# Two-layer decoder trunk on one core: the instruction order made with the framework's timeline simulation

## The chip, the cores and the metric

The kernel runs on one core of a Trainium2 chip, as one program with one launch. The metric is the device time in microseconds, as the median of several runs. A core has five engines with a queue of instructions each: TensorE (PE in the profile, with its weight loads as PEld), VectorE (DVE), ScalarE (ACT), GpSimd (POOL) and SyncE (SP). Each queue is worked off strictly in the order in which it was written into the program, and engines wait for each other by semaphores. SP and POOL also issue the DMA transfers here.

## The reference

The reference is a trunk of two layers on 512 tokens of width 1024. Layer 0 mixes tokens by multi-head latent attention, layer 1 by a gated linear recurrence (HGRN2). Cut to what matters:

```python
for i in range(2):
    h = mla_mixer(x, ...) if i % 2 == 0 else hgrn2_mixer(x, ...)
    x = layer_norm(ALPHA * x + h, ln_mix_g[i], ln_mix_b[i])
    hh = x @ ffn_w_in[i]                       # 1024 -> 2 * 2816
    g, u = hh[..., :2816], hh[..., 2816:]
    x = layer_norm(ALPHA * x + (silu(g) * u) @ ffn_w_down[i], ln_ffn_g[i], ln_ffn_b[i])
    x = x + sigmoid(x @ ple_w_gate[i]) * (p[i] @ ple_w_proj[i])
```

## The kernel before

Tokens lie in four tiles of 128 (NT), the width in eight chunks of 128 (KC). Every factor of a product is kept as two fp32r parts, a high part (`hi`, a rounded copy made by ACT in `split`, L179) and a low part (`lo`, source minus `hi`, made by DVE, L180, or for some weights by POOL), and `mm3` (L200 to L202) multiplies hi by hi, hi by lo and lo by hi.

The work of a layer runs in stages: the mixer; its output projection with the layer norm (`out_proj`, `ln_finish`, L330 to L344); the first product of the feed-forward part (`gate_up`); the second one (`ffn`, the "down" product); the gated embedding (`ple`).

`gate_up` handles 2 of the 22 column blocks in the plain way and 20 per layer (`block`, 40 in all) by a 2x2 block product with seven products in place of eight. One such product is 12 matmuls of 256 columns. In program order a block does: product into bank A; ACT copies A out (L439); product into B; product into C and its copy (L439); a further product accumulated into A, which must come after the copy of A was made; then more of the same kind. ACT and DVE also prepare the weights of the blocks to come (`prep`, L391 to L407): passes of ACT over 1024 columns (L184, L185, twice L179), and two over 512.

The down product (`ffn`) is such a block product too, over six blocks `b` of the inner dimension, five of size 2 and one of size 1, in the order 0, 1, 5, 2, 3, 4. Its first half makes, for each block, four weight operands: `b11` as it is, and `t1`, `t2`, `t3`, which are differences of the weight blocks made in a chain:

```python
r11 = load(0, 0, b)                                # L504, SP: DMA into a "raw" tile (3 slots)
...
t1 = mid(b, "ma")                                  # a tile of tag "ma" (5 slots)
minus(t1, r11, src(0, 1, b))                       # L509 ACT: t1 = -r11; L510 POOL: DMA adds a weight block to it
w1 = made(t1, b)                                   # L179 ACT, L180 DVE: its two parts (whi, wlo)
...
minus(t2, t1, src(1, 1, b))                        # L509, L510 again, on t1
w2 = made(t2, b)
...
t3 = mid(b, "ma")
v.tensor_tensor(out=t3, in0=t2, in1=r11, op=ALU.subtract)   # L558, DVE
w3 = made(t3, b)
```

So t1 needs a DMA that adds into it, t2 a second such DMA after the first has landed, and t3 needs t2. After that the block's 48 matmuls of 512 columns follow (24 in the block of size 1). The second half, which reuses t2, and the layer norm come behind. (The first t2 lies in a tile of tag "ma" as well and is held until the second half; the later ones have tiles of tag "big".)

What sets the order of the work: nobody writes it out. The kernel is traced as a program in the order of its Python code, and the framework's `TileContext` then makes the queues of all engines on leaving the `with` block. It plays the program through on a simulated machine; whenever an engine there is free, it takes the earliest instruction in program order whose inputs are there and for whose output tile a slot is free. An instruction may so pass earlier ones that are still waiting. In the order that came out for this kernel, instructions do pass each other on ACT, DVE, POOL and PE, but the first writers of the tiles of any one tag ("raw", "ma", "whi" and so on) stand in program order without an exception. On the chip the order is fixed; the semaphores that keep it right are put in by the framework.

Lines that the change and the prediction touch: L1099 (`TileContext`), L179, L180, L184, L185, L186, L200 to L202, L210, L304, L344, L439, L504, L509, L510, L558.

## Time and profile before

| | |
|---|---|
| median of 3 runs (lowest to highest) | 1341.29 us (1335.26 to 1345.14) |
| the profiled execution: its own time, its span | 1340.34 us, 1338.5 us |
| TensorE: matmuls busy, weight loads busy | 1267.8 us (95%), 1120.8 us (84%) |
| VectorE, ScalarE, GpSimd busy | 912.3, 751.9, 196.4 us (68%, 56%, 15%) |
| mean granted TensorE clock | 0.985 |
| moved by DMA | 173.77 MB, 130 GB/s on average |

A busy TensorE is not one at its peak: matmuls overlap, and one that waits inside its own record counts as busy. So a stage's speed is read from the number of matmuls in a stretch of time beside its busy time. The rows of a table by stretches give, in this order: the stretch, its length, the busy time and (in brackets) the count for PE, PEld, DVE, ACT and POOL, then the granted clock, the share of the DMA engines and the GB/s. A row of a timeline gives the start, the duration, the engine, the source line, the operation, output and input, and in square brackets the idle time before it with what ended it.

### The profile page before, as it was taken

How to read it: one execution, taken by the hardware profiler on the slowest of the kernel's cores; microseconds unless marked ns; L12 is line 12 of the kernel's file. 1: busy time of each engine (PE TensorE's matmuls, PEld its weight loads, DVE VectorE, ACT ScalarE, POOL GpSimd, SP SyncE). 2: the span in 40 equal slices, each digit the busy share in tenths (PEclk: the TensorE clock that was granted, in tenths of full speed). 3: DMA queues.
4: the chain of work that ended last, by engine and by line, in shares of the span. 5: the costliest groups of instructions: out<-in, count | busy, mean ns of one | idle time of the engine just before them, and what ended most of it. 6: DMA issues, size and time to landing. Idle time of an engine off the chain costs nothing.

```text
span 1338.5 us, 20202 instructions
## 1 busy us (share of the span) xinstructions
PE 1267.8 (95%) x7768; PEld 1120.8 (84%) x7768; DVE 912.3 (68%) x1608; ACT 751.9 (56%) x1276; POOL 196.4 (15%) x215
## 2 busy tenths in 40 slices
PE   8999999999999779899999999999999998978998
PEld 8787889999998558688888887889999998756787
DVE  7988397777757559843377776359677774747863
ACT  6666267776756557433334434247667765556652
POOL 0200131111211111100002220023211111111100
PEclk9999999999999889899999999999999999988999
DMA  6213128787876668421311221315887885676821
GB/s 221 80 48 127 62 65 205 186 192 174 184 161 118 113 142 228 146 96 63 127 63 63 64 87 35 99 63 152 212 180 182 186 185 110 114 127 154 236 95 48
DMA packets 53378, 173.77 MB, mean 130 GB/s; under 512 B 6305, under 2 KB 6561, under 8 KB 53025
## 3 DMA queue, kind: packets, MB, share of 16 engines
q1 hardware_dynamic: 34848, 117.94, 27.2%
q0 software_dynamic: 18432, 54.53, 23.8%
q8 instruction: 61, 1.00, 0.3%
q14 instruction: 37, 0.30, 0.1%
HBM read 170.35 MB, written 2.10 MB: 129 GB/s over the span
## 4 chain that ended last, share of the span: by engine, by line
PE 66%; DMA 10%; issue 9%; DVE 8%; ACT 5%; POOL 1%; SPq 0%; POOLq 0%; DVEq 0%; ACTq 0%
PE ps L200 16%; PE ps L201 16%; PE ps L202 16%; DMA big<-ffn_w_down 3%; DMA raw<-ffn_w_in 3%; PE sc L200 2%; PE sc L201 2%; PE wg L201 2%; PE sc L202 2%; PE wg L200 2%; PE wg L202 2%; DMA ma<-ffn_w_down 2%; DMA raw<-ple_w_proj 2%; PE tp L304 2%; PE sc L942 2%
## 5 line engine op out<-in xcount | busy, mean ns | idle before, releaser
L200 PE MATMUL ps<-big,whi 128*128 128x256 f32 (+1 forms) x768 | 237.3, 309 | 0.7 <-DVE part L459 0.7
L202 PE MATMUL ps<-big,wlo 128*128 128x256 f32 (+1 forms) x768 | 237.0, 309 | 0.0
L201 PE MATMUL ps<-big,whi 128*128 128x256 f32 (+1 forms) x768 | 235.8, 307 | 0.0
L200 PE MATMUL ps<-whi,big 128*128 128x512 f32 (+2 forms) x528 | 208.6, 395 | 6.2 <-ACT whi L179 6.2
L201 PE MATMUL ps<-wlo,big 128*128 128x512 f32 (+2 forms) x528 | 205.8, 390 | 4.0 <-DVE wlo L180 3.9
L202 PE MATMUL ps<-whi,big 128*128 128x512 f32 (+2 forms) x528 | 205.1, 388 | 0.0
L179 ACT ACTIVATE whi<-raw 128x1024 fp32r<-128x1024 f32 (+1 forms) x103 | 104.7, 1022 | 102.3 <-PE ps L202 35.7
L180 DVE TENSOR_TENSOR wlo<-raw,whi 128x1024 fp32r<-128x1024 f32 (+1 forms) x91 | 108.3, 1192 | 73.5 <-ACT whi L179 71.9
L200 PEld LDWEIGHTS ps<-big,whi 128*128 128x128 f32 x768 | 147.3, 192 | 5.7 <-DVE part L459 0.9
L201 PEld LDWEIGHTS ps<-big,whi 128*128 128x128 f32 x768 | 147.2, 192 | 5.4
L202 PEld LDWEIGHTS ps<-big,wlo 128*128 128x128 f32 x768 | 147.1, 192 | 5.2
L180 DVE TENSOR_TENSOR wlo<-ma,whi 128x1024 fp32r<-128x1024 f32 (+1 forms) x68 | 81.1, 1192 | 64.0 <-ACT whi L179 64.0
L200 PEld LDWEIGHTS ps<-whi,big 128*128 128x128 f32 x528 | 101.1, 192 | 26.2 <-ACT whi L179 8.3
L201 PEld LDWEIGHTS ps<-wlo,big 128*128 128x128 f32 x528 | 101.2, 192 | 25.4 <-DVE wlo L180 7.4
L202 PEld LDWEIGHTS ps<-whi,big 128*128 128x128 f32 x528 | 100.8, 191 | 19.1
L179 ACT ACTIVATE whi<-ma 128x1024 fp32r<-128x1024 f32 (+1 forms) x68 | 69.7, 1025 | 39.4 <-DMA ma<-ffn_w_down 28.7
L186 POOL DMA_DIRECT2D ma<-ffn_w_in x40 | 34.7, 869 | 233.6 <-DVE big L460 144.1
L210 POOL TENSOR_TENSOR rr<-rv,mhalf 128x1 f32<-128x1 f32 (+2 forms) x28 | 26.7, 952 | 235.7 <-DVE rv L208 235.7
L200 PE MATMUL sc<-whi,big 128*128 128x512 f32 (+1 forms) x104 | 42.1, 408 | 14.6 <-ACT whi L179 14.6
L439 ACT ACTIVATE part<-ps 128x256 f32<-128x256 f32 x120 | 44.0, 372 | 20.1 <-PE ps L202 20.1
L180 DVE TENSOR_TENSOR mb<-ma,mb 128x1024 fp32r<-128x1024 f32 x40 | 48.9, 1223 | 6.3 <-ACT mb L179 3.4
L180 POOL TENSOR_TENSOR wlo<-raw,whi 128x1024 fp32r<-128x1024 f32 x12 | 29.6, 2475 | 152.1 <-ACT whi L179 152.1
(329 smaller groups left out, 3222.5 us busy)
## 6 DMA issues: line engine op xcount, KB each, us to landing
raw<-ffn_w_in SPq DMA_DIRECT2D x88, 512.0 KB, 4.7
wlo<-ffn_w_in POOLq DMA_DIRECT2D x40, 512.0 KB, 7.1
raw<-ffn_w_down SPq DMA_DIRECT2D x30, 512.0 KB, 4.1
ma<-ffn_w_in POOLq DMA_DIRECT2D x40, 256.0 KB, 6.8
mb<-ffn_w_down POOLq DMA_DIRECT2D x20, 512.0 KB, 6.3
raw<-ple_w_gate SPq DMA_DIRECT2D x16, 512.0 KB, 3.5
raw<-hgrn_w_fq SPq DMA_DIRECT2D x16, 512.0 KB, 3.5
ma<-ffn_w_down POOLq DMA_DIRECT2D x12, 512.0 KB, 5.6
```

Source lines behind the costliest of these rows:

```text
L179: self.nc.scalar.activation(hi, src, AF.Copy)
L180: (eng or self.nc.vector).tensor_tensor(out=lo, in0=src, in1=hi.bitcast(F32), op=ALU.subtract)
L186: self.nc.gpsimd.dma_start(lo, src, accum_op=ALU.add)
L200: mm(ps, a[0], b[0], start=start, stop=False, skip_group_check=more)
L201: mm(ps, a[0], b[1], start=False, stop=False, skip_group_check=more)
L202: mm(ps, a[1], b[0], start=False, stop=stop, skip_group_check=more)
L210: nc.gpsimd.tensor_tensor(out=r, in0=v, in1=self.mhalf[:, :n], op=ALU.pow)
L304: self.nc.tensor.transpose(out=ps[:, c * P:(c + 1) * P], in_=src[:, c * P:(c + 1) * P], identity=self.ident)
L439: copy = lambda dst, src: nc.scalar.activation(dst, src[:, :N], AF.Copy)
L942: nc.tensor.matmul(ps[:, c * P:(c + 1) * P], X[:, c * P:(c + 1) * P], pair_view(cs[0][:, :, 1, :], cs[1][:, :, 0, :]), start=True, stop=True)
```

## The change

One argument of `TileContext` is added. It tells the framework to play the program through on another simulated machine, its timeline simulation, when it makes the queues. The traced program is the same: the same instructions with the same operands, tiles, tags and numbers of slots, in the same program order. What may differ is the order of the instructions on each engine, and with it the semaphores and the slot that each tile gets.

```diff
-    with tile.TileContext(nc) as tc:
+    with tile.TileContext(nc, schedule_with_timeline_sim=True) as tc:
         trunk(tc, ins, out)
```

## The prediction

> **What bounds the kernel now.** I read the page from the top, then the chain of waits, then tables by stretches, to see in which stage time is lost at all.
>
> ```profile
> PE 1267.8 (95%) x7768; PEld 1120.8 (84%) x7768; DVE 912.3 (68%) x1608; ACT 751.9 (56%) x1276; POOL 196.4 (15%) x215
> ...
> PEclk9999999999999889899999999999999999988999
> ...
> PE 66%; DMA 10%; issue 9%; DVE 8%; ACT 5%; POOL 1%; SPq 0%; POOLq 0%; DVEq 0%; ACTq 0%
> ```
>
> TensorE is the bound: 95% busy, two thirds of the chain that ended last. A new order adds and removes no work, so it can only shorten or lengthen the rest: time in which PE starves. Where is that? The table by stretches compares stages in which nothing but PE counts with the down product's first half:
>
> ```profile
> 267.60:368.10 100.50, 100.50 (x840) 100.50 (x839) 74.70 (x124) 71.29 (x122) 17.70 (x21) 1.00 0.81 184
> 970.30:1104.20 133.90, 133.90 (x1118) 133.90 (x1117) 100.32 (x165) 93.74 (x161) 22.64 (x26) 1.00 0.81 184
> 635.74:669.20 33.46, 33.46 (x149) 27.74 (x148) 11.89 (x11) 12.61 (x16) 0.00 (x0) 1.00 0.39 127
> 440.00:500.00 60.00, 45.58 (x161) 33.16 (x160) 32.35 (x43) 34.10 (x45) 8.68 (x10) 0.89 0.66 132
> 1160.00:1220.00 60.00, 45.50 (x167) 33.59 (x166) 30.43 (x40) 31.26 (x41) 9.56 (x11) 0.88 0.64 122
> ```
>
> The first two rows are the block products of gate_up in both layers: PE is busy throughout, with a matmul of 256 columns every 100.50 / 840 = 0.120 us, while DVE and ACT are busy 74% and 71%. No order makes this faster. The third row, plain products of 512 columns, gives PE's pace there: 33.46 / 149 = 0.225 us. The last two rows are the down product's first half, also 512 columns: 161 matmuls at that pace need 36.2 of the 60 us, 167 need 37.6. So PE loses 23.8 + 22.4 = 46.2 us in these two stretches, about a third of it (13.8 us, the 0.11 and 0.12 missing from the clock times 60) as a lower clock. That is the one large loss which an order could touch.
>
> **Why PE starves there.** DVE's timeline has the instruction that makes t3 (L558), once for each block:
>
> ```profile
> 442.31 0.69 DVE L558 TENSOR_TENSOR ma<-big,raw 128x512 f32<-128x512 f32 x1 [1.79 <-DMA big<-ffn_w_down]
> 458.31 1.23 DVE L558 TENSOR_TENSOR ma<-big,raw 128x1024 f32<-128x1024 f32 x1 [5.52 <-DMA big<-ffn_w_down]
> 474.18 1.23 DVE L558 TENSOR_TENSOR ma<-big,raw 128x1024 f32<-128x1024 f32 x1 [4.87 <-DMA big<-ffn_w_down]
> 491.58 1.23 DVE L558 TENSOR_TENSOR ma<-big,raw 128x1024 f32<-128x1024 f32 x1 [7.14 <-DMA big<-ffn_w_down]
> ```
>
> The period is 16.0, 15.9 and 17.4 us, where 48 matmuls need 10.8. ACT's and POOL's timelines show what fills one period:
>
> ```profile
> 442.37 0.63 ACT L179 ACTIVATE whi<-big 128x512 fp32r<-128x512 f32 x1 [2.99 <-DMA big<-ffn_w_down]
> 442.90 1.04 ACT L509 ACTIVATE ma<-raw 128x1024 f32<-128x1024 f32 x1
> 444.35 0.87 POOL L510 DMA_DIRECT2D ma<-ffn_w_down  x1 [5.18 <-DVE t L543]
> 450.48 1.06 ACT L179 ACTIVATE whi<-ma 128x1024 fp32r<-128x1024 f32 x1 [3.97 <-DMA ma<-ffn_w_down]
> 451.44 1.04 ACT L509 ACTIVATE big<-ma 128x1024 f32<-128x1024 f32 x1
> 452.89 0.87 POOL L510 DMA_DIRECT2D big<-ffn_w_down  x1 [5.12 <-DVE wlo L180]
> 458.31 1.06 ACT L179 ACTIVATE whi<-big 128x1024 fp32r<-128x1024 f32 x1 [2.24 <-DMA big<-ffn_w_down]
> 459.28 1.04 ACT L509 ACTIVATE ma<-raw 128x1024 f32<-128x1024 f32 x1
> ```
>
> Two adding DMAs stand one behind the other: t1 is negated at 442.90 and landed at 450.48; t2 is negated at 451.44 and landed at 458.31; then the next block's t1 is negated at 459.28. Between the blocks nothing overlaps. The reason is the tag "ma": t1 of the next block and t3 of this one come from it, t3 stands earlier in the program, and the first writers of a tag keep program order. So the next t1 can't start before L558 has its turn, and L558 waits for t2's DMA. Both simulated machines hand out slots from the same program, so I take this chain to survive the change.
>
> **The change part by part.** No instruction is added or removed, so the sum is made of displacements, against the profiled execution's own 1340.34 us (span 1338.5 us; 0.95 us under the median).
>
> *Saturated stages* (gate_up's blocks, the row products, HGRN): 0. What hides a displaced pass there is PE's queue of further products; the price if that cover goes is the second rival.
>
> *The chain in the down product*: the same instructions in the same chain, 0. What a new order could still do is swap ACT's two passes at each landing. Above, t2's negation starts 451.44 - 450.48 = 0.96 us after t1 has landed and the next t1's 459.28 - 458.31 = 0.97 us after t2, because the split of the landed weight goes first. Three full periods in each of two layers, 1.93 us each: 11.6 us gained if both negations go first everywhere, and a bound of +12.7 us (two passes of 1.06 us in six periods) if another pass is put ahead each time. The earlier instruction wins where both are ready, and both become ready with the same landing; so 0, with -11.6 and +12.7 kept for the range.
>
> *Borders at the layer norms*: here PE waits for one vector instruction after another.
>
> ```profile
> PE tp L304 <- DVE big L344: 10.3, 6, 3.9
> ...
> L180 DVE TENSOR_TENSOR wlo<-raw,whi 128x1024 fp32r<-128x1024 f32 (+1 forms) x91 | 108.3, 1192 | 73.5 <-ACT whi L179 71.9
> ...
> L661 ACT ACT_TABLE_LOAD x2 | 2.6, 1283 | 7.8 <-PE ps L202 7.8
> ```
>
> PE's transposes wait 10.3 us in all, in six places, for the layer norm's last step; that is what a perfect order could save. A weight split of 1.19 us that slips ahead in each of the six costs 7.2 us. Such a slip frees the weights of the stage behind earlier by as much, so I set 0 between -10.3 and +7.2. ACT's function tables are reloaded where functions mix, 1.28 us each; the trace has eight loads, and I bound what a new mix adds by four, 0 to +5.1, and take 0. Queues of SP and POOL: SP's loads are issued in program order, tag "raw", and stay; POOL's adding DMAs go with the chain above.
>
> **The sum** is 1340.3 + 0, or 1341 at the median's level, between 1340.3 - 11.6 - 10.3 = 1318 and 1340.3 + 12.7 + 7.2 + 5.1 = 1365 if all terms fall on one side.
>
> **The rivals.**
>
> *Faster: the chains overlap.* If the timeline simulation lets a later block's t1 start before this block's t3, the stage falls to PE's pace: -46.2, 1294 us. For it: raw tiles are loaded well ahead, and ACT stands idle 3.97 and 2.24 us in the rows above. Against it: the slots' order, and the transfers. In the stretch in which t1 lands, the DMA engines are full:
>
> ```profile
> 445.00:451.50 6.50, 1.75 (x7) 0.86 (x6) 2.07 (x4) 2.50 (x4) 1.07 (x2) 1.00 0.98 202
> 451.50:458.50 7.00, 6.30 (x14) 4.64 (x15) 1.41 (x2) 4.73 (x8) 1.75 (x2) 0.52 0.61 99
> ```
>
> A share of 0.98 at 202 GB/s: a block's four transfers of 512 KB (r11, and the weight blocks added into the low part of b11, into t1 and into t2) take 2.1 MB / 202 GB/s = 10.4 us, no less than PE's 10.8. [...]
>
> A smaller form: the gaps only get shorter, and the clock stays up. The next rows are the end of one burst of matmuls and the start of the next.
>
> ```profile
> 446.36 0.39 PE L202 MATMUL wg<-whi,big 128*128 128x512 f32 x1
> 451.59 0.65 PE L200 MATMUL sc<-whi,big 128*128 128x512 f32 x1 [4.84 <-ACT whi L179]
> ```
>
> After PE stood still for 4.84 us, the clock was 0.52 in the 7 us that follow. Without such gaps the 13.8 us of lost clock return: 1327 us. [...] I give both forms together 0.15.
>
> *Slower: gate_up loses its saturation.* Bank A must be copied out before the second product goes into it. In program order two products lie between, 24 x 0.120 = 2.9 us of cover. ACT's timeline in a block:
>
> ```profile
> 304.14 1.06 ACT L184 ACTIVATE whi<-raw 128x1024 fp32r<-128x1024 f32 x1
> 305.10 0.40 ACT L464 ACTIVATE part<-part 128x256 f32<-128x256 f32 x1
> 305.41 1.05 ACT L185 ACTIVATE wlo<-whi 128x1024 fp32r<-128x1024 f32 x1
> 306.36 0.36 ACT L439 ACTIVATE part<-ps 128x256 f32<-128x256 f32 x1
> 306.62 1.05 ACT L179 ACTIVATE mb<-ma 128x1024 fp32r<-128x1024 f32 x1
> 307.57 1.04 ACT L179 ACTIVATE whi<-ma 128x1024 fp32r<-128x1024 f32 x1
> ```
>
> The long passes stand between the copies, two at a time at most. A copy behind two of them is there after 2 x 1.06 + 0.36 = 2.5 us, inside the cover; behind three it takes 3.5 us, and PE waits 0.7 us. That is the point from which this rival decides: three long passes in a row ahead of the copy. Each block has four of them, so an order that bunches a block's preparation reaches it. At 0.7 us in each of 40 blocks: +28, 1368 us; with all four ahead twice as much and more. For it: PE's order is fixed as well, so a copy that is late on the chip can't be bypassed there. Against it: ACT is idle 29% of that stage, so passes need not bunch, and the simulated machine would see its own PE starve. 0.25.
>
> *The change does not do what it says*: dependencies and slots leave so little freedom that both machines give nearly the same queues: 1340 to 1342. For it: every tag keeps program order. Against it: between those fixed points instructions do pass each other now. 0.1.
>
> **How the numbers follow.** My forecast (terms that partly cancel, within 1318 to 1365) has 0.5: inside it 0.1 for faster by over 1% (13.4 us, under 1327.9), 0.32 within 1%, 0.08 slower. About 1% is what a measurement of this kernel can tell from no change: the three runs lie 0.7% apart. The overlap adds 0.12 to faster and 0.03 to same, the lost saturation 0.22 to slower and 0.03 to same, the unchanged order 0.1 to same: faster 0.22, same 0.48, slower 0.30. The predicted time is the forecast's, 1341 us. The range runs from 1315, just under the forecast's lower end, which leaves out the full overlap (0.08), to 1380, which takes in the third pass per block and leaves out a fourth one (0.1). The forecast's own range is 1318 to 1365.
>
> **What would show it.** Right: L558 again every 16 us, PE 0.120 us a matmul through gate_up, PEclk below full in the same down stretches, the layer norms' waits within a few us. The overlap would show as L509 on a raw tile before the L558 of the block ahead, and as a period near 11 us; the lost saturation as idle time of PE at L200 released by ACT L439 in gate_up, and fewer than 840 matmuls in 100 us. Most likely to make this wrong: that the timeline simulation fills an engine's queue further ahead than the default does, and so reverses priorities at places that I priced at nothing, the start (a stage that lives on loads) and the softmax among them.

## The result and the profile after

The changed kernel takes 1399.23 us (median of 4 runs, 1392.05 to 1400.54) against 1342.25 us for the kernel before (4 runs): ratio 1.0422, 95% interval 1.0368 to 1.0475. It is slower by 4.2%, and lies 19 us above the upper end of the predicted range. The profiled execution took 1400.54 us, its span is 1398.8 us.

The page of the kernel after, with PE's busy time and its granted clock in 40 slices:

```profile
PE 1290.1 (92%) x7768; PEld 1146.4 (82%) x7768; DVE 914.4 (65%) x1608; ACT 746.6 (53%) x1276; POOL 200.2 (14%) x215
...
PEclk9999999999999899999999998999999999989999
```

The same 7768 matmuls, 1608 DVE and 1276 ACT instructions are there: the order alone did this. PE's busy time grew by 1290.1 - 1267.8 = 22.3 us, its idle time by (1398.8 - 1290.1) - (1338.5 - 1267.8) = 38.0 us; together they are the 60.3 us of span. The busy part is clock: the mean granted clock fell from 0.985 to 0.965, which over the two spans is 20.1 and 49.0 us of clock withheld. By the trace's clock intervals and matmul records 16.9 and 41.0 us of it fell on a busy PE, and that part alone I count as loss. So about two fifths of the loss, 24.1 of 60.3 us, came through the clock.

Where it went is read from the stages. I cut both traces at the same instructions: the first and last exponential of the softmax (L822), the first and last copy of bank A in each gate_up (L439), the first copy of the gated embedding (L655), the first and last ACT copy ahead of a scan level of HGRN (L937), and its first Silu (L995). The lengths in us, with those of four experiments told of below (E1: queue of 4 for PE; E3: products tied; E7: queue of 1 for PE; E8: 4 for PE, 2 for the others). In two experiments, E6 and E7, one run of four took over 3200 us; their times here are the medians of the other three.

| stage | before | after | E1 | E3 | E7 | E8 |
|---|---|---|---|---|---|---|
| start to softmax | 66.0 | 67.5 | 66.8 | 66.5 | 81.8 | 65.9 |
| softmax | 68.9 | 81.4 | 68.8 | 79.8 | 103.2 | 66.6 |
| output projection, layer norm | 77.0 | 81.6 | 75.1 | 81.6 | 99.1 | 73.8 |
| gate_up, layer 0 | 204.5 | 202.7 | 201.2 | 202.1 | 215.9 | 201.9 |
| down product, layer 0 | 142.4 | 142.6 | 137.0 | 137.2 | 163.6 | 131.1 |
| embedding, HGRN's values | 124.9 | 124.4 | 124.0 | 124.4 | 122.6 | 126.1 |
| HGRN's scan | 127.4 | 162.9 | 124.7 | 136.1 | 166.9 | 124.7 |
| end of the scan | 12.9 | 18.8 | 15.2 | 21.5 | 19.3 | 15.2 |
| gate, output projection, layer norm | 109.0 | 116.9 | 110.6 | 117.5 | 133.8 | 108.8 |
| gate_up, layer 1 | 206.7 | 202.7 | 200.8 | 204.8 | 216.9 | 200.9 |
| down product, layer 1 | 139.8 | 138.8 | 137.8 | 138.3 | 162.7 | 130.4 |
| the rest | 59.2 | 58.7 | 58.4 | 58.7 | 56.9 | 60.5 |

HGRN's scan and its end take 41.4 us more, the softmax 12.5, the two borders 4.6 and 7.9; gate_up and the down product take 6.6 us less.

**HGRN.** Its code, cut to the lines that matter: for each of four pairs of heads come projections, 96 long products for each pair that wait for nothing of the scan, and then seven levels of a scan, each of which needs DVE's result of the level ahead.

```python
for p in range(H // 2):                                  # four pairs of heads
    for hh in range(2):
        for q in range(2):
            for kc in range(KC):
                self.mm3(ps, ...)                        # L912: 24 products of 512 columns
    ...
    for lev in range(NLEV):                              # seven levels
        a_.activation(..X.., both(K, w, 0), AF.Copy)     # L937, ACT
        nc.tensor.matmul(ps[...], X[...], ...)           # L942, PE: 8 short matmuls
        v_.tensor_tensor(out=kv, ...); v_.tensor_tensor(out=qv, ...)   # L949, L950, DVE
```

PE's timeline of one pair in the kernel before, the matmuls of the scan levels alone:

```profile
724.20 1.15 PE L942 MATMUL sc<-ma,t 128*128 128x128 f32 x8
...
726.35 1.07 PE L942 MATMUL sc<-ma,t 128*128 128x128 f32 x8
...
737.57 1.05 PE L942 MATMUL sc<-ma,t 128*128 128x128 f32 x8
```

Seven levels, one every 2.2 us ((737.57 - 724.20) / 6), and in the left-out rows 5, 4, 4, 5, 6 and 6 of the matmuls between two levels are products of the next pair (L200 to L202): they fill just the time in which DVE and ACT make the next level ready. Another 66 stand between the last level and the next pair's first. The same in the kernel after, with the steps behind the scan:

```profile
712.26 1.08 PE L942 MATMUL sc<-big,t 128*128 128x128 f32 x8
...
719.33 1.08 PE L942 MATMUL sc<-big,t 128*128 128x128 f32 x8
...
725.95 1.06 PE L942 MATMUL sc<-big,t 128*128 128x128 f32 x8
...
730.49 1.06 PE L942 MATMUL sc<-big,t 128*128 128x128 f32 x8
...
736.60 1.16 PE L942 MATMUL sc<-big,t 128*128 128x128 f32 x8
739.29 0.71 PE L979 MATMUL wg<-big,big 128*128 128x128 f32 x4 [1.52 <-DVE big L950]
...
745.30 1.22 PE L979 MATMUL wg<-big,big 128*128 128x128 f32 x4 [4.18 <-DVE big L988]
```

The first levels stand 7.1, 6.6 and 4.5 us apart, with 27, 25 and 16 products between them where a few would do. At the fourth level the products are used up, and what follows runs bare. The bare levels are not slower than the filled ones, 2.0 us apart ((736.60 - 730.49) / 3); the loss lies behind them, at the output steps (L979): PE waits 1.52 and 4.18 us, and four short matmuls after the second wait take 1.22 us in place of 0.71. In this pair only 40 products are left behind the last level. By stretches (length, busy time and count of PE, PEld, DVE, ACT, POOL, then granted clock, DMA share, GB/s), the scan before and after:

```profile
683.60:811.00 127.40, 123.94 (x732) 103.72 (x730) 99.76 (x175) 49.38 (x113) 22.72 (x27) 1.00 0.20 63
```
```profile
700.10:863.00 162.90, 137.29 (x745) 118.64 (x743) 98.68 (x169) 49.29 (x113) 23.16 (x27) 0.94 0.15 49
```

PE does about the same number of matmuls and idles 25.6 us in place of 3.5; the clock falls to 0.94, and 0.06 x 162.9 = 9.8 us are withheld. PE's longest waits in these stretches, before and after (who waits for what: us in total, times, longest):

```profile
PE sc L942 <- ACT t L937: 1.9, 8, 0.3
PE wg L979 <- DVE big L988: 1.5, 3, 0.5
```
```profile
PE wg L979 <- DVE big L988: 12.5, 3, 4.2
PE wg L979 <- DVE big L950: 3.0, 2, 1.5
PE wg L979 <- DVE ma L950: 2.1, 1, 2.1
```

So 17.6 of the 25.6 us are waits of the output steps behind the last level, and not waits of the levels. The products spent on the first levels are missing there.

**The softmax and the border behind it.** From the start to gate_up, before and after:

```profile
66.00:134.90 68.90, 67.23 (x407) 55.16 (x407) 59.78 (x189) 44.20 (x130) 2.40 (x1) 1.00 0.25 88
...
0.00:211.90 211.90, 201.17 (x1211) 174.92 (x1212) 166.28 (x417) 125.25 (x264) 32.47 (x36) 1.00 0.33 103
```
```profile
67.50:148.90 81.40, 77.85 (x451) 65.36 (x451) 57.44 (x189) 44.04 (x128) 2.39 (x1) 0.98 0.17 64
...
0.00:230.50 230.50, 212.61 (x1234) 185.39 (x1235) 168.14 (x421) 129.16 (x267) 33.83 (x36) 0.96 0.31 98
```

The softmax's stretch holds 44 matmuls more, so part of its 12.5 us is work moved into it. Over the whole start that nearly evens out (1234 against 1211 matmuls), and 18.6 us of loss remain: 7.2 more idle, and 9.2 us withheld by a clock of 0.96. The clock falls mostly at the border (0.92 from 148.9 to 230.5, against 0.98 in the softmax). PE's timeline there, in the kernel after:

```profile
189.28 0.63 PE L200 MATMUL ps<-big,whi 128*128 128x256 f32 x3 [0.77 <-ACT big L179]
...
190.71 0.39 PE L200 MATMUL sc<-big,whi 128*128 128x256 f32 x1 [0.80 <-ACT whi L184]
193.03 0.58 PE L201 MATMUL ps<-big,whi 128*128 128x256 f32 x1 [1.93 <-DVE big L180]
```

The transposes wait for the layer norm no longer; the products behind them wait for the parts of what was transposed and for a weight, one short wait after another. The last section shows what the longest of them hangs on.

**What stayed.** A stretch of gate_up and the down product's L558, in the kernel after:

```profile
250.00:350.50 100.50, 100.50 (x839) 100.50 (x839) 74.08 (x121) 67.74 (x119) 17.17 (x20) 1.00 0.81 184
```
```profile
457.58 0.69 DVE L558 TENSOR_TENSOR ma<-big,raw 128x512 f32<-128x512 f32 x1 [0.69 <-DMA big<-ffn_w_down]
474.61 1.23 DVE L558 TENSOR_TENSOR ma<-big,raw 128x1024 f32<-128x1024 f32 x1 [3.32 <-DMA big<-ffn_w_down]
491.41 1.23 DVE L558 TENSOR_TENSOR ma<-big,raw 128x1024 f32<-128x1024 f32 x1 [0.81 <-DMA big<-ffn_w_down]
507.90 1.23 DVE L558 TENSOR_TENSOR ma<-big,raw 128x1024 f32<-128x1024 f32 x1 [4.48 <-DMA big<-ffn_w_down]
```

839 matmuls in 100.5 us, where there were 840, and for L558 a period of 17.0, 16.8 and 16.5 us.

### The profile page after: what moved, and what is told of

It reads as the page before. It is cut to its first block, busy times and chain, and to the rows that moved or that the text cites. A ratio compares the mean times of both kernels' runs of the same rounds, so it can differ in the third digit from the quotient of the medians.

```text
span 1398.8 us, 20173 instructions
## 1 busy us (share of the span) xinstructions
PE 1290.1 (92%) x7768; PEld 1146.4 (82%) x7768; DVE 914.4 (65%) x1608; ACT 746.6 (53%) x1276; POOL 200.2 (14%) x215
## 5 line engine op out<-in xcount | busy, mean ns | idle before, releaser
L200 PE MATMUL ps<-big,whi 128*128 128x256 f32 (+1 forms) x768 | 241.2, 315 | 8.5 <-ACT part L439 3.6
L201 PE MATMUL ps<-big,whi 128*128 128x256 f32 (+1 forms) x768 | 240.3, 313 | 5.5 <-DVE big L180 5.5
L202 PE MATMUL ps<-big,wlo 128*128 128x256 f32 (+1 forms) x768 | 239.2, 312 | 0.0
L200 PE MATMUL ps<-whi,big 128*128 128x512 f32 (+2 forms) x528 | 204.0, 393 | 15.0 <-ACT whi L179 7.6
L202 PE MATMUL ps<-whi,big 128*128 128x512 f32 (+2 forms) x528 | 203.0, 389 | 0.0
L200 PEld LDWEIGHTS ps<-big,whi 128*128 128x128 f32 x768 | 151.4, 197 | 16.4 <-ACT part L439 4.0
L201 PEld LDWEIGHTS ps<-big,whi 128*128 128x128 f32 x768 | 152.0, 198 | 11.9 <-DVE big L180 6.3
L202 PEld LDWEIGHTS ps<-big,wlo 128*128 128x128 f32 x768 | 151.8, 198 | 6.3
L180 DVE TENSOR_TENSOR wlo<-raw,whi 128x1024 fp32r<-128x1024 f32 (+1 forms) x91 | 108.9, 1201 | 72.9 <-ACT whi L179 71.3
L200 PEld LDWEIGHTS ps<-whi,big 128*128 128x128 f32 x528 | 100.4, 191 | 37.3 <-ACT whi L179 9.2
L180 DVE TENSOR_TENSOR wlo<-ma,whi 128x1024 fp32r<-128x1024 f32 (+1 forms) x68 | 81.0, 1192 | 58.7 <-ACT whi L179 58.7
L202 PEld LDWEIGHTS ps<-whi,big 128*128 128x128 f32 x528 | 101.2, 192 | 19.2
L439 ACT ACTIVATE part<-ps 128x256 f32<-128x256 f32 x120 | 41.6, 375 | 47.6 <-PE ps L202 47.6
L180 DVE TENSOR_TENSOR mb<-ma,mb 128x1024 fp32r<-128x1024 f32 x40 | 48.9, 1221 | 10.9 <-PE ps L201 7.2
L180 DVE TENSOR_TENSOR big<-big,big 128x512 fp32r<-128x512 f32 x68 | 45.0, 688 | 15.5 <-PE ps L201 5.9
L186 POOL DMA_DIRECT2D wlo<-ffn_w_in x40 | 34.8, 871 | 133.2 <-ACT part L439 53.3
```

Of the source, the lines that this page charges most:

```text
L180: (eng or self.nc.vector).tensor_tensor(out=lo, in0=src, in1=hi.bitcast(F32), op=ALU.subtract)
L186: self.nc.gpsimd.dma_start(lo, src, accum_op=ALU.add)
L200: mm(ps, a[0], b[0], start=start, stop=False, skip_group_check=more)
L201: mm(ps, a[0], b[1], start=False, stop=False, skip_group_check=more)
L202: mm(ps, a[1], b[0], start=False, stop=stop, skip_group_check=more)
L439: copy = lambda dst, src: nc.scalar.activation(dst, src[:, :N], AF.Copy)
```

## The experiments

**The theory.** The timeline simulation gives each engine an issue queue, into which instructions go ahead of their turn. On its PE that queue holds 35, a number set in the framework. As soon as a long product's inputs are there it goes in, and a scan level, ready only later, lands behind whatever is queued: the products that should cover seven levels and the steps behind them are spent on the first three. **The rivals**: the order on ACT and DVE is to blame; or it is something else of this simulation, its durations for instance, and not the queue. The depths are plain numbers of the simulated machine and can be set in the kernel's file; nothing of the chip changes with them, and what the chip's own queues hold no run shows.

**E1: a queue of 4 for PE.** The edit, ahead of the kernel's function:

```diff
+from concourse.hw_specs import TRN2Spec
+TRN2Spec.ENG_ISSUE_QUEUE_DEPTH = {**TRN2Spec.ENG_ISSUE_QUEUE_DEPTH, mybir.EngineType.PE: 4}
```

> One number of the simulated machine is changed: TensorE's issue queue holds 4 instructions there instead of 35; the order is still made with the timeline simulation. Theory (the simulated TensorE takes its instructions too far ahead, so the products that should fill the gaps of a chain are spent in front of it): the HGRN scans fall from 162.9 us back to about 127, the softmax stage and the borders lose most of their extra 12 and 18 us, and the total is 1342, between 1330 and 1355. Rival (the orders on ScalarE and VectorE do the harm): their queues are unchanged, so the total stays at 1385 to 1400.

1320.83 us, ratio 0.9882 (0.9862 to 0.9902). HGRN's scan by stretches:

```profile
672.80:797.50 124.70, 124.70 (x754) 110.44 (x753) 100.23 (x174) 49.68 (x113) 16.02 (x27) 1.00 0.19 64
```

PE has no idle time in it and the clock is full. In the order on PE, 7 to 13 products stand between two levels. The softmax is at 68.8 us and the first border at 75.1. The scan, the softmax and the first border are as short as before or shorter, by one number (the scan's end and the second border keep 2.3 and 1.6 us of the loss). The whole comes out 1.2% faster than the kernel before, under the expected range: gate_up takes 9.2 us less in the two layers and the down product 7.4. What shortens these two was not followed.

**E2: queues of 2 for ACT, DVE and POOL, PE as it was.**

```diff
+TRN2Spec.ENG_ISSUE_QUEUE_DEPTH = {**TRN2Spec.ENG_ISSUE_QUEUE_DEPTH,
+    mybir.EngineType.Activation: 2, mybir.EngineType.DVE: 2, mybir.EngineType.Pool: 2}
```

> The counterpart: in the simulated machine the issue queues of ScalarE, VectorE and GpSimd hold 2 instructions instead of 12, TensorE's keeps 35. Theory: the products in front of the HGRN scans stay where they are, so the total stays at 1385 to 1405. Rival: 1340 to 1355.

1390.55 us, ratio 1.0404 (1.0384 to 1.0424). HGRN takes 162.9 us as in the kernel after, the softmax 80.2 against 81.4; only the first border falls, from 81.6 to 75.4. So the first rival falls for HGRN and the softmax. At that border either change of depth is enough, since E1 brings it to 75.1 as well.

**E3: the changed kernel with HGRN's products tied.** Ties that order instructions without a wait put the products of pairs 1 to 3 behind steps of the pair ahead of them: six between two levels, and half of the 96 behind the last level (6 at once, 18 behind the output step of the pair's first head, 24 behind that of the second). Nothing else in the program is touched. Cut to what matters:

```diff
+    def behind(self, ins, other):
+        if other is not None:
+            self.tc.add_manual_dep(ins.ins, other.ins.name, ...NoSync..., reason="pace")
...
-                        self.mm3(ps, ..., kc == 0, kc == KC - 1)
+                        head = self.mm3(ps, ..., kc == 0, kc == KC - 1)
+                        self.behind(head, pace.get((2 * hh + q) * KC + kc))
...
+                    pace[4 + 2 * lev] = nc.tensor.matmul(ps[...], ...)      # a scan level
...
+                        last = nc.tensor.matmul(op[:, ts], ...)             # a head's output step
+                pace[(18, 24)[hh]] = last
```

> The change as it is, with TensorE's queue of 35 in the simulated machine; only in HGRN the projection products of the next pair of heads are tied, in TensorE's order alone, behind the levels of the scan of this pair (6 matmuls between two levels). Nothing ties the last pair. Theory: the first three pairs, 55.1, 48.2 and 41.7 us in the changed kernel, fall to about 38 each (37.4 before), the total by 28 to 33 us to 1366 to 1372; softmax and borders stay. Rival (ScalarE's and VectorE's order): the levels stay as slow as they are whatever stands between them, total 1390 to 1402.

1371.68 us, ratio 1.0255 (1.0231 to 1.0278), in the range expected. The scan takes 136.1 us, 26.8 less than in the kernel after, with the queue of 35 left in place:

```profile
691.60:827.60 136.00, 130.07 (x745) 110.07 (x743) 97.43 (x169) 49.71 (x112) 16.59 (x27) 1.00 0.18 59
```

The clock is full again, and the first three pairs take 39.4, 38.3 and 38.3 us, as expected. Where the products stand, between the levels and behind them, is thus the mechanism, and by E1 the queue is what misplaces them. Which of the two places counts for more E3 does not separate; the waits of the changed kernel put more on the one behind.

**E4: the kernel before with the products bunched.** The default machine again; the products of the later pairs get a higher priority, so that they go first.

```diff
-                    for kc in range(KC):
-                        self.mm3(ps, ...)
+                    with self.tc.high_priority(400 if p else 0):
+                        for kc in range(KC):
+                            self.mm3(ps, ...)
```

> The kernel before, order made with the default model; only the HGRN projection products of a later pair get a higher priority, so that they are taken in front of the scan instead of between its levels (72 in a row, then bare levels, in the first two pairs). Theory: the scans lose their filling and the total rises by 20 to 35 us, to 1362 to 1377. Rival: TensorE's order alone costs less than 5 us, total 1340 to 1347.

1383.71 us, ratio 1.0364 (1.0334 to 1.0394): a scan about as long as the changed kernel's 162.9 us, without the timeline simulation. The embedding's stage and the scan by stretches:

```profile
558.50:696.30 137.80, 137.04 (x630) 112.95 (x629) 56.53 (x74) 51.15 (x72) 1.95 (x3) 1.00 0.28 95
```
```profile
696.30:857.40 161.10, 130.95 (x702) 110.86 (x702) 99.97 (x171) 45.63 (x109) 24.86 (x34) 0.92 0.14 46
```

The products left the scan for the stage ahead (12.9 us longer, at a full clock), and the scan still got 33.7 us longer with 30 matmuls fewer than before. My size, 1362 to 1377, was too small: the priority pulled products further forward than the changed kernel does.

**E5, E6, E7: queues of 12, 64 and 1 for PE.** The edit is E1's line with the other number.

> Timeline simulation with TensorE's issue queue at 12 (4 gave a ratio of 0.988, 35 gave 1.042). 9 to 16 products now stand between two scan levels, and in the last pair the last levels are bare. Theory (the loss grows with the depth): HGRN scan 130 to 138 us, softmax 69 to 73, total 1325 to 1340. If something else than the depth makes the loss (that 4 is a lucky order), the total need not lie between the two.

1359.19 us, ratio 1.0149 (1.0111 to 1.0186): scan 141.4, softmax 75.1 us. Between 4 and 35 as the theory has it, but higher than expected. Nine to fifteen products stand between two levels of the first pair and none between the last levels of the last one, as foreseen; but PE's longest waits in the scan are again those of L979 for L988, 6.5 us in two, which the expectation had not counted.

> The same with TensorE's queue at 64, deeper than in the change: 41, 28 and 24 products in front of the first levels, all later levels bare. Theory: HGRN scan 163 to 178 us, softmax 80 to 90, total 1398 to 1425.

1425.85 us, ratio 1.0654 (1.059 to 1.0718), the total 0.9 us above the range expected and the scan at 171.6 us inside its own. The softmax, at 80.1 us, does not grow beyond the changed kernel's 81.4.

> The same with TensorE's queue at 1. Of all depths its order is nearest to that of the kernel before, but only 3 products stand between two levels (5 before) and the last levels are bare, since 79 products are left for the end of a pair. Theory: a level costs about 2 us whatever stands in it (before: 1.9 us with 4 to 6 products), so TensorE waits and HGRN takes 10 to 20 us more than at 4, 135 to 145 us; the rest as at 4; total 1330 to 1342. So the best depth is not the least.

1544.96 us, ratio 1.1542 (1.15 to 1.1583): a plain miss. It isn't HGRN alone (three products between the first levels, then none, and up to 5.3 us for a level where I had counted about 2); the table above has a loss in ten of twelve stages. PE's waits of this kernel, the longest in total:

```profile
PE ps L200 <- ACT part L439: 28.6, 39, 3.6
PE tp L304 <- DVE big L344: 28.0, 4, 12.2
PE ps L200 <- DVE ma L573: 21.3, 6, 5.2
PE sc L942 <- ACT t L937: 17.9, 8, 3.5
```

So "shorter is better" holds only down to a point. The first row is the wait of the prediction's slower rival, a product in bank A behind a late copy: 28.6 us in 39 waits, 0.73 each on average.

**E8: 4 for PE and 2 for the others.** E1's and E2's edits together.

> TensorE's queue at 4 and those of ScalarE, VectorE and GpSimd at 2 in place of 12. Theory: these engines' depth mattered only at the border behind the attention (75.4 us with 2 beside TensorE's 35, 81.6 in the change), and that border is at 75.1 already with TensorE at 4, so this adds nothing: 1314 to 1325, same as at 4.

1309.03 us, ratio 0.978 (0.9744 to 0.9816): 2.2% faster than the kernel before. I had expected nothing beyond E1; the down products fell to 131.1 and 130.4 us, from 137.0 and 137.8 in E1.

**E9 and E10: which engine's queue that was.** 4 for PE, and 2 for ACT alone, then for DVE alone.

> The timeline simulation with an issue queue of 4 for PE, as in the first experiment (1320.83 us), and of 2 for ACT alone. With 2 on ACT, DVE and POOL together the down product took 131.1 and 130.4 us in place of 137.0 and 137.8. Theory: that gain is ACT's order alone, because the negations (L509) and the splits (L179) which begin the chain of a block are ACT's: the down product falls to 130 to 133 us in both layers, the whole to 1307 to 1313 us. Rival: it is DVE's order (t3 at L558 and the low parts at L180): nothing is gained here, 1318 to 1324 us.

1319.07 us, ratio 0.9844 (0.981 to 0.9879): as E1. My theory falls.

> The timeline simulation with an issue queue of 4 for PE and of 2 for DVE alone, the mirror of the run with 2 for ACT alone. If the gain in the down product is ACT's, the down product stays at 136 to 139 us in each layer and the whole at 1317 to 1324 us. If it is DVE's, the down product falls to 130 to 133 us and the whole to 1307 to 1313 us. If both are needed, this run and its mirror both stay above 1315 us.

1310.19 us, ratio 0.978 (0.9748 to 0.9812): all of E8's gain. The second half of layer 0's down product, from the last L558 to the end of the stage, before, in E9 and in E10:

```profile
491.60:558.70 67.10, 60.42 (x247) 48.46 (x248) 60.14 (x93) 44.74 (x61) 7.72 (x9) 0.90 0.68 191
```
```profile
487.60:548.60 61.00, 58.26 (x251) 46.89 (x252) 57.35 (x88) 42.14 (x57) 6.34 (x7) 0.95 0.65 191
```
```profile
483.50:540.70 57.20, 55.99 (x237) 45.65 (x238) 52.96 (x81) 41.22 (x54) 7.27 (x8) 0.94 0.74 214
```

DVE is the fullest engine beside PE here: 60.14 of 67.10, 57.35 of 61.00 and 52.96 of 57.20 us. The stretch shortens as DVE's instructions in it go from 93 to 88 and 81. That the depth of DVE's simulated queue makes the gain is shown. That it works through DVE's own order is not: with that depth the orders on PE and ACT change too. Where the missing instructions run I did not follow.

**E11 and E12: how short may the queues be?** 2 for PE beside 2 for the others; and 4 for PE beside 1 for the others.

> The best version so far (PE 4, the others 2: 1309.03 us) with 2 for PE as well. Theory: a shorter queue only keeps program order among PE's ready products, and the seven scan levels of HGRN already have products between them at 4, so the time is 1303 to 1315 us with 123 to 127 us in HGRN's scan. Rival, from the run with 1 for PE (1545.16 us): a simulated PE with few places feeds itself badly, so the order that it makes worsens step by step, and 2 gives 1340 to 1420 us, with three products or fewer between the scan levels.

1310.59 us, ratio 0.978 (0.9739 to 0.9821), scan 123.0 us: no worsening at 2.

> PE 4 with 1 for ACT, DVE and POOL. It tells whether a queue of 1 does harm on any engine or on PE alone. Theory: on PE alone, because PE has 7768 matmuls of a quarter of a microsecond or less, and the other engines fewer and longer instructions: 1305 to 1325 us. Rival: any engine whose next instruction is handed over only when the last is done loses in the simulated machine, so that passes of ACT and DVE drift behind PE's products everywhere: 1330 to 1450 us.

1313.02 us, ratio 0.9803 (0.9774 to 0.9832). A queue of 1 does no harm that shows on ACT, DVE and POOL. What E7 shows belongs to a PE queue of 1 (with 12 for the others); why its order is late everywhere is left open.

## Why the prediction was wrong, step by step

- **Saturated stages: 0.** This step failed, for HGRN. I took a stage in which PE is busy for one that any order keeps busy. gate_up is one: 839 matmuls in 100.5 us against 840. HGRN isn't: PE was busy because five products or so stood between any two scan levels and 66 behind the last one, and that is a property of the order. I wrote that "PE's queue of further products" hides a displaced pass, and did not ask how many there are and where they stand. It cost 35.5 us in the scan and 5.9 at its end, more than two thirds of the loss. In its place the runs show a stage whose idle time grows from 3.5 to 25.6 us when the products are spent on the first levels. E1, E3 and E4 show it from three sides.
- **The softmax** was not in the sum; the last sentence names it, with the mechanism that came true (a queue filled further ahead reverses priorities). That PE's queue does it the depths show: 68.8 us with 4 places, 75.1 with 12, 81.4 with 35. Which instructions pass which there was not followed. Part of its 12.5 us is moved work; from the start to gate_up the loss is 18.6 us.
- **Borders: 0, between -10.3 and +7.2.** They cost 4.6 and 7.9 us, 12.5 in all, outside the bound. The 10.3 us of the transposes' waits did go (no wait of L304 for L344 is left), but other waits took their place, and I priced a slip only as idle time. The larger part of the 12.5 us goes with the clock: it was 1.00 over both borders before and 0.92 and 0.97 after, 0.08 x 81.6 + 0.03 x 116.9 = 10.0 us withheld.
- **The down product: 0.** Right: 142.6 and 138.8 us against 142.4 and 139.8, L558 every 16.5 to 17.0 us, and the chain survived, as argued from the slots; no run changes the number of slots, so that they are the reason is not tested. What I did not see is how much the second half can give: in E10 it is 9.9 us shorter (67.1 to 57.2).
- **Table loads: 0, up to +5.1.** Right: eight of them, 1.28 us each, as before.
- **The rivals.** "The chains overlap" did not happen: one L558 after the other at the old distance. Nor did its smaller form: the clock over layer 0's down product was 0.93 before and is 0.92 after. How short a gap has to be for the clock to stay up no run shows; behind waits of 1.93 us and less it fell to 0.50 (last section). "gate_up loses its saturation" gave the right sign for the wrong reason: PE's waits for L439 fell here, from 10.9 to 4.5 us in all, while in E7 they came at 0.73 us on average, near the 0.7 that I had priced. "The change does not do what it says" is excluded: the order of PE is another from the first stages on.

## What to carry to other kernels

A busy engine is no proof that a stage bears any order: ask of each stage whether its instructions are ready at once (gate_up) or come one by one and are covered by others (a scan), and count the cover between two of them and behind the last. Where a simulation makes the order, the length of its issue queues decides how ready filler and late critical work are mixed: here 64, 35, 12 and 4 places on PE gave 1426, 1399, 1359 and 1321 us, 1 gave 1545, and 2 for DVE beside PE's 4 took another 1%. Look at the order that a planner made, and change its one number before its model is dropped.

## What the runs showed of the hardware

**The clock fell behind waits of 1.93 us and less.** Behind the first border of the kernel after (the rows at 189.28 to 193.03 above) PE's longest wait is 1.93 us. The next waits there:

```profile
211.07 0.38 PE L200 MATMUL ps<-big,whi 128*128 128x256 f32 x1 [0.43 <-ACT big L179]
212.00 0.72 PE L200 MATMUL ps<-big,whi 128*128 128x256 f32 x2 [0.54 <-DVE big L433]
213.53 0.58 PE L201 MATMUL ps<-big,whi 128*128 128x256 f32 x1 [0.82 <-DVE big L180]
```

By stretches, each place and what follows it:

```profile
189.90:193.00 3.10, 0.39 (x2) 0.19 (x1) 3.10 (x4) 1.82 (x2) 2.71 (x2) 0.89 0.44 155
193.00:199.00 6.00, 5.97 (x28) 5.97 (x29) 2.50 (x5) 1.20 (x2) 0.12 (x1) 0.50 0.71 164
211.50:214.10 2.60, 1.29 (x4) 0.94 (x5) 2.57 (x6) 1.12 (x4) 0.90 (x1) 0.75 0.92 222
214.10:220.00 5.90, 5.90 (x31) 5.90 (x30) 5.86 (x8) 2.01 (x3) 0.00 (x0) 0.53 0.51 126
```

In 3.1 us with 0.39 us of matmuls the clock goes down, and then 28 matmuls take 6 us, about half of gate_up's pace. At the second place the clock is 1.00 up to 212.8 and 0.51 from there, when of the waits shown only those of 0.43 and 0.54 us have passed. Eight transposes of 1.29 us in all stand right ahead of these; what part they have in it no run here shows. The six waits are 5.3 us in all, and the clock withheld behind them is 0.50 x 6.0 + 0.47 x 5.9 = 5.8 us: here the clock cost as much again as the waits.

The kernel before shows it too, without transposes. PE waited 1.17 us up to 1217.14 and 1.15 us up to 1218.79, and then:

```profile
1216.30:1219.80 3.50, 1.51 (x5) 1.05 (x6) 3.50 (x5) 3.30 (x6) 0.00 (x0) 1.00 0.44 117
1219.80:1223.20 3.40, 3.40 (x9) 2.64 (x8) 3.40 (x7) 3.40 (x8) 0.00 (x0) 0.50 0.27 59
```

Here the two waits of 1.17 and 1.15 us were followed by a clock of 0.50. The prediction's row had 4.84 us of standing still ahead of its 0.52; these rows show that the clock also fell after much shorter waits.

**A one-column instruction took 2.32 us.** The longest of those waits, 1.93 us, ended with DVE's split at 192.30. DVE's and POOL's timelines ahead of it:

```profile
189.40 2.32 DVE L333 TENSOR_TENSOR lnst<-lnst 128x1 f32<-128x1 f32 x1
...
192.30 0.68 DVE L180 TENSOR_TENSOR big<-tp,big 128x512 fp32r<-128x512 f32 x1
```
```profile
189.19 2.51 POOL L180 TENSOR_TENSOR wlo<-raw,whi 128x1024 fp32r<-128x1024 f32 x1
```

The instructions of that line, with the shortest, median and longest duration in ns:

```profile
L333 DVE TENSOR_TENSOR lnst<-lnst x16: 148/159/2320, 173.3 to 1340.7; 128x1 f32<-128x1 f32 x16
```

So one column takes 0.159 us as a rule. Here it ends at 191.72, as POOL's weight split does (191.70), and the split for which PE waits stands behind it. Neither of the two instructions reads what the other writes. In each of the two traces a weight split of POOL (L180) overlaps two of the 16 instructions of L333, one in each layer: these take 1.62 and 1.63 us before and 2.32 and 2.31 us after, and each ends 0.02 us behind a split of POOL's. The other 14 take 0.147 to 0.161 us. So L333 was long in all four cases beside such a split, here with PE waiting behind it. That the split holds it up is my reading of these times; by what means it would, no run shows.

This is not new with the change. DVE and POOL at the same border in the kernel before:

```profile
180.45 3.55 DVE L344 SCALAR_TENSOR_TENSOR big<-big,rr,ma 128x512 f32<-128x512 f32 x2
...
184.64 1.62 DVE L333 TENSOR_TENSOR lnst<-lnst 128x1 f32<-128x1 f32 x1
...
186.37 1.28 DVE L180 TENSOR_TENSOR big<-tp,big 128x512 fp32r<-128x512 f32 x2
```
```profile
181.03 7.59 POOL L180 TENSOR_TENSOR wlo<-raw,whi 128x1024 fp32r<-128x1024 f32 x3 [0.75 <-ACT whi L179]
```

Beside POOL's three splits two instructions of L344, 0.75 us each as a rule, take 3.55 us together (0.75 and 2.89), and L333 takes 1.62; the two of L180, which read the transposes' result (`tp`), take 0.68 each, as they do elsewhere. So the long instructions beside POOL's splits do not by themselves explain the loss at the border: both kernels have them, and the new order only changes which instructions they are. No experiment took this wait away by itself.
